# TensorE issues one stage of a hybrid decoder in the order of tracing: the MLP of the last layer's first token group, beside the end of an RWKV-7 recurrence

## The chip, the cores and the metric

One core of a Trainium2 chip runs the whole kernel. The metric is device time in microseconds (us) of one execution. A core has a matrix engine (TensorE, PE in the profile; its weight loads are listed apart as PEld), a vector engine (VectorE, DVE), a scalar engine (ScalarE, ACT), a general engine (GpSimd, POOL) and a queue engine (SyncE, SP). They run beside each other, each through its own list of instructions, strictly in the order of that list, and wait for one another by semaphores. An instruction that waits holds everything behind it on its engine.

## The reference

The model has two layers over 1040 prompt tokens (1024 and 16 learned ones put ahead of them) and 8 single decode tokens, with 1024 features. Layer 0 mixes tokens by a convolution, layer 1 by the RWKV-7 recurrence; each is followed by an MLP with 4096 hidden features. What matters here is the second layer from its recurrence on:

```
def _wkv7_step(S, inp):
    r_t, w_t, k_t, v_t, kk_t, a_t = inp
    sa = jnp.einsum('bhvk,bhk->bhv', S, -kk_t)
    S = (S * w_t[:, :, None, :] + sa[..., None] * (kk_t * a_t)[:, :, None, :]
         + v_t[..., None] * k_t[:, :, None, :])
    y = jnp.einsum('bhvk,bhk->bhv', S, r_t)
    return S, y
...
    yn = ((y - mu) * lax.rsqrt(var + GN_EPS)).reshape(B, T, D_MODEL)
...
    out = ((yn + bonus).astype(h.dtype) * g) @ w_o
...
def _sqrelu_mlp(h, w_in, w_out):
    return jnp.square(jax.nn.relu(h @ w_in)) @ w_out
```

There are 16 heads of 64 x 64 states. The 8 decode tokens take one step each from states that are inputs.

## The kernel before, in words

Features lie on the 128 partitions, tokens along the free axis. Every large product is done in three passes: activations and weights are split into a high and a low part, and high x high, high x low and low x high are summed in PSUM (L187, L188, L189). One output block of 128 features, called a column here, takes 8 blocks of input features times 3 passes, 24 matmuls of 128x128 weights by the tokens of a group. `dense` issues them. ScalarE casts the raw weights to the high part (L157), GpSimd subtracts for the low part (L162).

The recurrence goes in chunks of 64 tokens. A chunk is a chain of small products on TensorE with VectorE, ScalarE and GpSimd between them: A (L1168, products within the chunk), gg and po (L1206, in 32x32 pieces), W (L1236), U (L1252), S (L1261, the new state) and Y (L1268, L1271, the outputs), and transposes bT (L1229). gg, po, W, U and S are 16 matmuls each, Y is 32. Each piece needs the vector work on the piece before it: `w` (L1238), `p` (L1245), `uv` (L1253, L1254), `sv` (L1282). Triangular inverses for four chunks at a time are made on VectorE (`inverses`, L1127 and L1128). After the chunks `norm_gate` normalises and gates the outputs and writes them to `d_z` in DRAM, where the output projection reads them (transposes `yn`, L1388).

The last layer's output projection and MLP go by token groups. The stage in question is that of the first, 328 tokens, and it starts before the recurrence has ended: chunks 12 to 16 are still to come. `mixer_out` (L1441 on) loads the eight z parts (L1449), splits them into high and low (L140, L141), runs eight columns of the projection (`ps_oo`) and adds them to the residual (L1453). Then `mlp` (L300 on) takes the row sums (`st_m`, L231), the normalised input `m_h`, `m_l` (L269, L270), 32 columns of the first product (`ps_in`; on VectorE `r`, L327) and 16 x 8 blocks of the second (`out`, added to `h` at L340).

Between them stands other work. At fixed points (half-way through `dense`, after a column, after an `out` block) the code calls `fill`, which draws the next pieces from two streams at set rates: the recurrence (`until`), and the decode step followed by the norm gates. `decode_step` (L1317 on) first transposes the decode tokens' vectors on TensorE (`pdd`, L1327), copies them (L1330), writes them to `d_dec` and reads them back as `dq` (L1334), and then does 16 pieces of nine VectorE operations each (L1349 to L1357) on states loaded by SP's queue (L1346).

All of that gives the order of tracing. It isn't yet the order of the engines: the framework plays the traced program against a model of the engines, and each engine's instructions are issued in the order in which that model would start them, by readiness and by priority (the recurrence's priority is raised in `until`). So in before the pieces of the recurrence stand wherever the model had them ready, often one small matmul between two dense ones. Accumulators are PSUM banks from pools of fixed size (4 for the dense products, 3 for the recurrence, 1 for the others); weights pass through 5 raw buffers and 5 split ones.

Of the kernel before, what the change touches and what calls it, by code (L numbers as in the profile page):

```python
# [48 lines left out]
def hybrid_step(tc, x_prompt, x_sample, state_conv, state_shift, state_wkv, meta_tokens,  # L49
# [8 lines left out]
    nc = tc.nc  # L58
    ctx = ExitStack()
    with ctx:  # L60
# [77 lines left out]
        def split(hi, lo, src, eng_lo):  # L138

            nc.scalar.copy(hi, src)  # L140
            eng_lo.tensor_sub(lo, src, hi.bitcast(F32))  # L141
# [7 lines left out]
        def load_w(src, shape, name, eng_lo, tag="w", raw=None):  # L149

            a, b = shape
            if raw is None:
                raw = load_raw(src, shape, name)
            nb = cur["bufs"][tag]
            hi = cur["wsp"].tile([P, 8 * P], F32R, name=f"{name}_hi", tag=tag + "h", bufs=nb)
            lo = cur["wsp"].tile([P, 8 * P], F32R, name=f"{name}_lo", tag=tag + "l", bufs=nb)
            nc.scalar.copy(hi[:, :a * b], raw[:, :a * b])  # L157

            step = 2 * P if eng_lo is nc.gpsimd else a * b
            for c in range(0, a * b, step):  # L160
                cs = slice(c, min(c + step, a * b))
                eng_lo.tensor_sub(lo[:, cs], raw[:, cs], hi[:, cs].bitcast(F32))  # L162
            v = lambda t: t[:, :a * b].rearrange("p (a b) -> p a b", a=a)
            return v(hi), v(lo)
# [5 lines left out]
        def load_col(w, m, name, eng_lo, tag="w"):  # L170
            return load_w(col_src(w, m), (KT, P), name, eng_lo, tag)
# [13 lines left out]
        def mm3(ps, w, act, first, last):  # L185

            nc.tensor.matmul(ps, w[0], act[0], start=first, stop=False)  # L187
            nc.tensor.matmul(ps, w[1], act[0], start=False, stop=False)  # L188
            nc.tensor.matmul(ps, w[0], act[1], start=False, stop=last)  # L189

        def bank(name, tag="mm"):
            return cur[tag].tile([P, 512], F32, name=name, tag=tag)

        def dense(w, act, n, name, fill=None):
            ps = bank(f"ps_{name}")
            for k in range(KT):
                mm3(ps[:, :n], (w[0][:, k, :], w[1][:, k, :]), (act[0][:, k, :n], act[1][:, k, :n]), k == 0, k == KT - 1)
                if fill and k == KT // 2 - 1:
                    fill()
            return ps  # L200
# [5 lines left out]
        def tt(name, tag):  # L206
            return cur["tmp"].tile([P, cur["n"]], F32, name=name, tag=tag)
# [95 lines left out]
        def mlp(layer, groups, lag, eng_w, eng_h, fill=None, done=None):  # L303


            w_in, w_out = w_mlp_in[layer], w_mlp_out[layer]
            nj = DFF // P
            hid = {}

            def load_in(j):  # L310
                return load_col(w_in, j, f"wi{layer}_{groups[0][0]}_{j}", eng_w)

            def load_out(b):

                for i in range(2):
                    src = w_out[2 * b * P:(2 * b + 2) * P, i * 4 * P:(i + 1) * 4 * P].rearrange("(j p) c -> p j c", p=P)
                    yield load_w(src, (2, 4 * P), f"wo{layer}_{groups[0][0]}_{b}_{i}", eng_w)

            def inp(j, w, group):
                gn, hv, n, ah, al, rs, hid_pool = group  # L320
                if j % 2 == 0:
                    hid[gn, j // 2] = [hid_pool.tile([P, 2, cur["wide"]], F32R, name=f"h{q}{layer}{gn}_{j}", tag=f"h{q}") for q in "hl"]
                hh, hl = hid[gn, j // 2]
                ps = dense(w, (ah, al), n, f"in{layer}_{j}_{gn}", fill)
                with tc.high_priority(offset=HR):
                    r = tt(f"r{layer}_{j}_{gn}", "t1")
                    nc.vector.scalar_tensor_tensor(r[:, :n], ps[:, :n], 0.0, rs[:, :n], op0=ALU.max, op1=ALU.mult)  # L327
                    s = tt(f"s{layer}_{j}_{gn}", "t2")
                    nc.scalar.activation(s[:, :n], r[:, :n], AF.Square)  # L329
                    split(hh[:, j % 2, :n], hl[:, j % 2, :n], s[:, :n], eng_h)  # L330

            def out(b, i, w, group):
                gn, hv, n, ah, al, rs, hid_pool = group
                hh, hl = hid[gn, b]
                for m in range(4):
                    ps = bank(f"out{layer}_{b}_{gn}_{4 * i + m}")
                    for j in range(2):
                        mm3(ps[:, :n], [part[:, j, m * P:(m + 1) * P] for part in w], (hh[:, j, :n], hl[:, j, :n]), j == 0, j == 1)
                    with tc.high_priority(offset=HA):
                        nc.vector.tensor_add(hv[:, 4 * i + m, :], hv[:, 4 * i + m, :], ps[:, :n])  # L340
                    if fill:
                        fill()

            def outs(b):
                for i, w in enumerate(load_out(b)):
                    for group in groups:
                        out(b, i, w, group)

            last = nj - 1
            for j in range(last):  # L350
                w = load_in(j)
                for group in groups:
                    inp(j, w, group)
                b, odd = divmod(j - lag, 2)
                if b >= 0 and odd:
                    outs(b)
                if fill:
                    fill()
            for b in range((last - lag) // 2, nj // 2 - 1):
                outs(b)  # L360
            w, wo = load_in(last), list(load_out(nj // 2 - 1))
            for group in groups:
                inp(last, w, group)
                for i in range(2):
                    out(nj // 2 - 1, i, wo[i], group)
                if done and group is not groups[-1]:
                    done(group[0])

        with ExitStack() as l0:
# [6 lines left out]
            actp = [pool(l0, f"actp0{i}", 1) for i in range(2)]  # L376
            residp = [pool(l0, "resid00", 1)]
# [253 lines left out]
            with ExitStack() as s:  # L631
# [3 lines left out]
                fill, rest = filler(8 * KT, ([ranked(CV0, conv(0)), ranked(CV0, ln_silu(0))], EARLY * (15 * KT // 2 + 2 + 2 * MW + KT)))  # L635
# [43 lines left out]
            hidp = pool(l0, "hidp0", 2)  # L679
# [751 lines left out]
        with ExitStack() as l1:  # L1431
            open_weights(l1, 5, {"w": 5}, "f")
            open_tmp(l1, N2, "2", 3)
            residp = pool(l1, "resid1", 1)
            actp = pool(l1, "actp1", 1)
            hidp = pool(l1, "hidp1", 2)
# [5 lines left out]
            def mixer_out(g, residp, actp, fill, add):  # L1442
                lo, n = G2[g]
                h1 = hl[g] = residp.tile([P, KT, cur["wide"]], F32, name=f"h1_{g}", tag="h")
                nc.sync.dma_start(h1[:, :, :n], d_h[:, :, lo:lo + n])
                z = new_act(actp, f"z{g}", cur["wide"])
                for p in range(KT):
                    t = tt(f"zr{g}{p}", "t1")
                    nc.sync.dma_start(t[:, :n], d_z[:, p, lo:lo + n])  # L1449
                    split(z[0][:, p, :n], z[1][:, p, :n], t[:, :n], nc.vector)  # L1450
                for m in range(KT):
                    ps = dense(load_col(rwkv_w_o[0], m, f"wo{g}_{m}", nc.gpsimd), z, n, f"oo{g}_{m}", fill)
                    nc.vector.tensor_add(h1[:, m, :n], h1[:, m, :n], ps[:, :n])  # L1453
                    add(m, h1[:, m, :n])
                    fill()
# [57 lines left out]
            def group(g, actp, hidp, sums):  # L1513
                n = G2[g][1]
                hv = hl[g][:, :, :n]
                return (g, hv, n, *mlp_in(actp, hv, n, 1, f"m1{g}", sums), hidp)
# [3 lines left out]
            fill, rest = filler(2 * KT + MLP_POINTS,  # L1520
                                ([until(NCH - 1)], FA * CHUNK_WAIT * (NCH - 1 - st["done"])),
                                ([decode_step(), norm_gates(GN_OF[1]), ng2], NGA))
            add, sums = sums_of(0)
            mixer_out(0, residp, actp, fill, add)
            mlp(1, [group(0, actp, hidp, sums)], 2, nc.gpsimd, nc.vector, fill)
            for _ in rest:
                pass
            lw.close()
            outp = pool(l1, "outp", 1)
            cur["wide"] = max(n for lo, n in G2[1:])  # L1530
# [2 lines left out]
            fill, rest = filler(2 * KT, ([ng2], NGB))  # L1533
            add, sums = sums_of(1)
# [6 lines left out]
            fill, rest = filler(2 * KT + MLP2_POINTS, ([ranked(FN, final(0))], FB))  # L1541
            add, sums = sums_of(2)
# [3 lines left out]
            def done(g):  # L1546
                end.append(filler(KT, ([final(g)], 24)))
# [38 lines left out]
```

## Time and profile before

| | us |
|---|---|
| three runs | 2887.63, 2895.84, 2894.62; median 2894.62 |
| the profiled execution | 2896.42 |
| its span (first to last instruction) | 2894.7 |
| the changed stage in it, from the first `ps_oo` matmul to that of the next group | 1855.5 to 2313.7 |
| the mixing stage ahead of it, as counted in the text | 1236 to 1849 |

Times in rows count from the start of the span. A row of the timeline has start, duration, engine, line, operation, output and inputs by the program's names, shape and number of equal instructions in a row; what stands in brackets is the idle time before it and what ended it. Matmuls overlap in their pipeline, so the time that one costs is the distance between two starts, not its duration. The granted clock (PEclk) is the share of TensorE's full speed that it was allowed in that stretch.

### The profile page before, as it was taken

The page shows a single profiled execution, that of the slowest core. Times are in us where ns is not written, and L with a number is a line of the kernel's source. Part 1 is how long each engine was busy: PE and PEld are TensorE (multiplying, and loading weights), DVE is VectorE, ACT ScalarE, POOL GpSimd, SP SyncE. Part 2 cuts the span into 40 slices and gives each one's busy share as a digit, 9 for nine tenths or more (in the row PEclk, how much of TensorE's full clock was granted, in tenths as well). Part 3 has the DMA queues.
Part 4 walks back from the last instruction along what each step waited for, and adds up shares of the span by engine and source line. Part 5 has one row for each costly group of instructions (what it writes and reads, how often), then busy time and mean ns, then how long its engine had stood idle before and what let it go on. Part 6 is the DMA issues. An engine that isn't in the chain of part 4 may idle for free.

```text
span 2894.7 us, 51574 instructions
## 1 busy us (share of the span) xinstructions
PE 2781.4 (96%) x19594; PEld 2573.7 (89%) x19594; DVE 1785.7 (62%) x3618; ACT 1187.1 (41%) x2233; POOL 1436.8 (50%) x1983
## 2 busy tenths in 40 slices
PE   8999999999999899999999999879999999999998
PEld 8988999999999898777877877777779999999998
DVE  5999999994454544336765555597345654444444
ACT  5546444543454332333445444443234552222223
POOL 6677778887788772000100111365246883343432
PEclk9999999999999999999999999889899999999999
DMA  6563544454444643687767767854336642222211
GB/s 181 171 184 95 154 139 132 137 178 138 138 145 146 189 151 109 183 213 202 183 184 202 180 159 181 206 143 126 95 109 198 192 148 87 70 66 74 66 59 41
DMA packets 649654, 416.42 MB, mean 144 GB/s; under 512 B 126184, under 2 KB 600360, under 8 KB 649406
## 3 DMA queue, kind: packets, MB, share of 16 engines
q1 hardware_dynamic: 643164, 410.20, 50.3%
q10 hardware_dynamic: 6018, 2.89, 0.4%
q8 instruction: 155, 2.54, 0.4%
q14 instruction: 93, 0.76, 0.1%
q0 software_dynamic: 224, 0.03, 0.0%
HBM read 345.60 MB, written 68.37 MB: 143 GB/s over the span
## 4 chain that ended last, share of the span: by engine, by line
PE 75%; DVE 9%; POOL 6%; DMA 4%; issue 3%; ACT 2%; SPq 0%; DVEq 0%; ACTq 0%; POOLq 0%
PE out L187 7%; PE out L189 7%; PE out L188 7%; PE ps_in L187 7%; PE ps_in L189 7%; PE ps_in L188 7%; PE pk L845 4%; POOL wo_lo L162 3%; PE pr L845 3%; PE pv L845 3%; POOL wi_lo L162 2%; PE A L1168 2%; DVE cv L504 1%; PE U L1252 1%; PE ps_g L187 1%
## 5 line engine op out<-in xcount | busy, mean ns | idle before, releaser
L162 POOL TENSOR_TENSOR wo_lo<-wo_raw,wo_hi 128x256 fp32r<-128x256 f32 x736 | 565.3, 800 | 329.6 <-ACT wo_hi L157 301.6
L162 POOL TENSOR_TENSOR wi_lo<-wi_raw,wi_hi 128x256 fp32r<-128x256 f32 x640 | 489.0, 796 | 293.6 <-ACT wi_hi L157 253.0
L187 PE MATMUL out<-hh,wo_hi 128*128 128x352 f32 (+2 forms) x1536 | 507.2, 330 | 20.4 <-DVE r L327 9.0
L340 DVE TENSOR_TENSOR h<-h,out 128x352 f32<-128x352 f32 (+2 forms) x768 | 386.4, 510 | 220.4 <-PE out L189 219.9
L187 PE MATMUL ps_in<-m_h,wi_hi 128*128 128x352 f32 (+2 forms) x1536 | 502.4, 327 | 12.7 <-ACT m_h L269 12.1
L189 PE MATMUL out<-hl,wo_hi 128*128 128x352 f32 (+2 forms) x1536 | 497.8, 327 | 5.6 <-DVE hl L141 5.6
L188 PE MATMUL out<-hh,wo_lo 128*128 128x352 f32 (+2 forms) x1536 | 502.1, 327 | 0.0
L188 PE MATMUL ps_in<-m_h,wi_lo 128*128 128x352 f32 (+2 forms) x1536 | 501.2, 327 | 0.0
L189 PE MATMUL ps_in<-m_l,wi_hi 128*128 128x352 f32 (+2 forms) x1536 | 500.4, 326 | 0.0
L504 DVE SCALAR_TENSOR_TENSOR cv<-u,wdw,cv 128x352 f32<-128x352 f32 (+2 forms) x720 | 376.9, 573 | 0.7
L157 ACT CAST wi_hi<-wi_raw 128x1024 fp32r<-128x1024 f32 x160 | 168.0, 1050 | 399.9 <-PE out L189 191.7
L157 ACT CAST wo_hi<-wo_raw 128x1024 fp32r<-128x1024 f32 x184 | 192.9, 1050 | 321.6 <-PE out L189 158.4
L187 PEld LDWEIGHTS out<-hh,wo_hi 128*128 128x128 f32 x1536 | 293.7, 191 | 28.3 <-DVE h L340 11.0
L187 PEld LDWEIGHTS ps_in<-m_h,wi_hi 128*128 128x128 f32 x1536 | 292.4, 190 | 17.1 <-ACT m_h L269 12.5
L189 PEld LDWEIGHTS out<-hl,wo_hi 128*128 128x128 f32 x1536 | 292.9, 192 | 9.4 <-DVE hl L141 7.1
L188 PEld LDWEIGHTS out<-hh,wo_lo 128*128 128x128 f32 x1536 | 293.6, 191 | 2.9
L189 PEld LDWEIGHTS ps_in<-m_l,wi_hi 128*128 128x128 f32 x1536 | 292.3, 190 | 2.9
L188 PEld LDWEIGHTS ps_in<-m_h,wi_lo 128*128 128x128 f32 x1536 | 291.9, 190 | 3.0
L327 DVE SCALAR_TENSOR_TENSOR r<-ps_in,rs_m 128x352 f32<-128x352 f32 (+2 forms) x192 | 98.5, 515 | 263.7 <-PE ps_in L189 260.0
L141 DVE TENSOR_TENSOR hl<-s,hh 128x352 fp32r<-128x352 f32 (+2 forms) x192 | 140.4, 732 | 99.4 <-ACT hh L140 99.1
L329 ACT ACTIVATE s<-r 128x352 f32<-128x352 f32 (+2 forms) x192 | 93.9, 491 | 133.0 <-DVE r L327 132.8
L845 PE MATMUL pv<-mx,wv_raw 128*128 128x256 f32 (+2 forms) x512 | 124.9, 398 | 5.5 <-ACT rk L1029 5.5
(350 smaller groups left out, 4925.3 us busy)
## 6 DMA issues: line engine op xcount, KB each, us to landing
wi_raw<-in_w_mlp_in_dram SPq DMA_DIRECT2D x160, 512.0 KB
wo_raw<-in_w_mlp_out_dram SPq DMA_DIRECT2D x160, 512.0 KB
wk_raw<-in_rwkv_w_k_dram SPq DMA_DIRECT2D x32, 512.0 KB
wr_raw<-in_rwkv_w_r_dram SPq DMA_DIRECT2D x32, 512.0 KB
wv_raw<-in_rwkv_w_v_dram SPq DMA_DIRECT2D x32, 512.0 KB
d_ab<-ab SPq DMA_DIRECT2D x32, 512.0 KB
pg_raw<-in_conv_w_pw_dram SPq DMA_DIRECT2D x24, 512.0 KB
pa_raw<-in_conv_w_pw_dram SPq DMA_DIRECT2D x24, 512.0 KB
```

What stands on the lines that cost most here:

```text
L141: eng_lo.tensor_sub(lo, src, hi.bitcast(F32))
L157: nc.scalar.copy(hi[:, :a * b], raw[:, :a * b])
L162: eng_lo.tensor_sub(lo[:, cs], raw[:, cs], hi[:, cs].bitcast(F32))
L187: nc.tensor.matmul(ps, w[0], act[0], start=first, stop=False)
L188: nc.tensor.matmul(ps, w[1], act[0], start=False, stop=False)
L189: nc.tensor.matmul(ps, w[0], act[1], start=False, stop=last)
L327: nc.vector.scalar_tensor_tensor(r[:, :n], ps[:, :n], 0.0, rs[:, :n], op0=ALU.max, op1=ALU.mult)
L329: nc.scalar.activation(s[:, :n], r[:, :n], AF.Square)
L340: nc.vector.tensor_add(hv[:, 4 * i + m, :], hv[:, 4 * i + m, :], ps[:, :n])
L504: nc.vector.scalar_tensor_tensor(acc[m][:, :n], ug[:, m, j:j + n], wdw[:, m, j:j + 1], acc[m][:, :n], op0=ALU.mult, op1=ALU.add)
L845: nc.tensor.matmul(ps[:, :n], w[:, k, :], act[k], start=k == 0, stop=k == KT - 1)
L1168: nc.tensor.matmul(ps[:, i * 2 * P:(i + 1) * 2 * P], bk[:, j + i, :], xa[:, j + i].rearrange("p q x -> p (q x)"), start=True, stop=True)
```

## The change

The calls that trace the stage are put under `manual_schedule` for TensorE: its instructions of this stage are issued in the order in which they are traced. VectorE, ScalarE, GpSimd and the DMA queues are ordered by the model as before, and before and behind the stage so is TensorE.

```
             add, sums = sums_of(0)
-            mixer_out(0, residp, actp, fill, add)
-            mlp(1, [group(0, actp, hidp, sums)], 2, nc.gpsimd, nc.vector, fill)
-            for _ in rest:
-                pass
+            with tc.manual_schedule(engines={nc.tensor.engine}):
+                mixer_out(0, residp, actp, fill, add)
+                mlp(1, [group(0, actp, hidp, sums)], 2, nc.gpsimd, nc.vector, fill)
+                for _ in rest:
+                    pass
             lw.close()
```

The order of TensorE at the start of the stage becomes: half of column 0 of the projection; gg and bT of chunk 12 and the first two `pdd` transposes; the rest of column 0; half of column 1, two `pdd`, and so on to the last two `pdd` behind column 3; W, po, U, S and Y of chunk 12 each in one block between halves of columns; after column 7 the row sums, and only then the first product's columns, one after the other. In before, the first columns were taken side by side as the z parts came in, and the `pdd` transposes were issued in the stage ahead.

## The prediction

> **What bounds the kernel now.** I read the head of the page first, then the chain that ended last.
>
> ```profile
> span 2894.7 us, 51574 instructions
> PE 2781.4 (96%) x19594; PEld 2573.7 (89%) x19594; DVE 1785.7 (62%) x3618; ACT 1187.1 (41%) x2233; POOL 1436.8 (50%) x1983
> ...
> PE 75%; DVE 9%; POOL 6%; DMA 4%; issue 3%; ACT 2%; SPq 0%; DVEq 0%; ACTq 0%; POOLq 0%
> ```
>
> TensorE carries three quarters of the chain, so time taken from TensorE is time taken from the kernel, unless another engine is late there. But a busy TensorE need not be a fast one. The second view is the table by windows: the mixing stage ahead, then the changed stage in four parts. The columns are PE, PEld, DVE, ACT and POOL busy with their instructions, the granted clock, the DMA share and GB/s.
>
> ```profile
> 1236.00:1849.00 613.00, 582.85 (x5770) 479.81 (x5769) 352.91 (x863) 272.94 (x719) 67.86 (x149) 0.98 0.73 187
> 1871.70:1910.00 38.30, 33.99 (x268) 31.64 (x268) 36.98 (x82) 15.00 (x27) 22.61 (x26) 0.94 0.68 151
> 1910.00:2040.50 130.50, 119.75 (x805) 98.72 (x805) 106.05 (x221) 45.34 (x83) 68.33 (x82) 0.87 0.49 134
> 2040.50:2200.00 159.50, 159.50 (x1056) 121.42 (x1055) 64.61 (x132) 53.01 (x107) 58.22 (x72) 0.89 0.38 104
> 2200.00:2309.00 109.00, 107.97 (x720) 106.83 (x718) 72.41 (x129) 57.49 (x100) 92.95 (x117) 1.00 0.72 216
> ```
>
> Until 2040 the stage is shared: VectorE is busy 37.0 of 38.3 us, then 106 of 130.5, with the decode step and the chunk's inverses. From 2040 to 2200 TensorE is busy without a gap and yet passes 1056 matmuls in 159.5 us, fewer per us than in the last 109 us, which have none of the recurrence. All other engines are under half busy there. Why, the timeline of TensorE shows.
>
> ```profile
> 2085.08 0.31 PE L188 MATMUL out<-hh,wo_lo 128*128 128x328 f32 x1
> 2085.23 0.31 PE L189 MATMUL out<-hl,wo_hi 128*128 128x328 f32 x1
> ...
> 2086.32 0.33 PE L1236 MATMUL W<-sv,xa 128*64 128x64 f32 x2
> 2086.57 0.41 PE L188 MATMUL out<-hh,wo_lo 128*128 128x328 f32 x1
> 2086.92 0.33 PE L1236 MATMUL W<-sv,xa 128*64 128x64 f32 x2
> ...
> 2149.12 1.15 PE L1236 MATMUL W<-sv,xa 128*64 128x64 f32 x32
> 2150.20 0.69 PE L1206 MATMUL po<-p,gg 32*32 32x32 f32 x32
> ```
>
> Dense matmuls (128x328) start 0.15 us apart (2085.08, 2085.23). One small W instruction (two records) set between two dense ones makes the pair 0.60 us long (2086.32 to 2086.92). The same W's in one block (16 instructions, 32 records) take 2150.20 - 2149.12 = 1.08 us, 0.068 each. So a lone small matmul costs 0.60 - 0.15 - 0.07 = 0.38 us more than one in a block. At a low clock it is worse:
>
> ```profile
> 2003.81 0.64 PE L187 MATMUL out<-hh,wo_hi 128*128 128x328 f32 x1
> 2004.38 0.31 PE L1206 MATMUL gg<-x,no 32*32 32x32 f32 x2
> 2004.63 0.64 PE L188 MATMUL out<-hh,wo_lo 128*128 128x328 f32 x1
> ```
>
> The pair is now 0.82 us (2003.81 to 2004.63).
>
> **The change part by part.** No instruction is added or taken away: in the program's order each engine issues the same operations. What moves is TensorE's order; the other engines' orders are still the scheduler's and shift along with it. In tracing order each recurrence piece (gg, W, po, U, S, Y: 16 instructions each, Y 32) stands in one block, with some 70 dense matmuls between blocks, where before had them singly between dense ones. I split the stage at the first A product of chunk 15, behind which the same instructions are left in both orders.
>
> ```profile
> 2039.82 1.02 PE L1168 MATMUL A<-xa,bk 128*128 128x256 f32 x4
> ...
> 2313.72 0.32 PE L187 MATMUL ps_oo<-z_h,wo_hi 128*128 128x352 f32 x1
> ```
>
> *Second part*, from there to the next group's first matmul: 273.9 us in before. Its work, put together from rows:
>
> ```profile
> 1887.53 2.00 PE L1168 MATMUL A<-xa,bk 128*128 128x256 f32 x8
> 1889.18 0.50 PE L187 MATMUL ps_oo<-z_h,wo_hi 128*128 128x328 f32 x1
> ...
> 2146.49 0.60 PE L1388 MATMUL yn<-ident,ey 128*128 128x128 f32 x4
> ```
>
> 47 weight columns of 24 dense matmuls, 1128 x 0.15 = 169.2. S 48, Y 96, W 32, U 32 instructions, 208 x 0.068 = 14.1. gg and po, 64 at about 0.04 (the po row: 0.69 us with its tail for 16) = 2.6. A, 16 instructions, four of which (eight records) took 1889.18 - 1887.53 = 1.65 us: 6.6. Transposes (bT 16, yn 48, state 16) at about 0.11 ((0.60 - 0.27) / 3 in the yn row) = 8.8. Sum 201.3 us; 72.6 us of before are no work. The granted clock explains part of it: 0.89 over 159.5 us lacks 17.5 us of pulses. The other 55 are some 140 lone matmuls at 0.38.
>
> In blocks the 55 go. Two things stay. First, the clock: the mixing stage runs the same pieces in blocks, and it had 0.98 over 613 us and 12 chunks, 12 us or 1 a chunk. Here it is 0 at best and 17.5 at worst; I take 6, near the mixing row, since dense blocks keep TensorE as busy as in the last window (1.00). Second, waits: a piece that isn't ready now holds the dense matmuls behind it. Before shows few of them:
>
> ```profile
> PE S L1261 <- DVE uv L1253: 0.8, 1, 0.8
> PE gg L1206 <- DVE x L1182: 0.6, 1, 0.6
> ```
>
> With 70 dense matmuls (10 us) between blocks, and VectorE under half busy, an answer (a copy of under 1 us and an add) is mostly there; eight blocks at 0.5 give 4 (0 to 20). After: 201.3 + 6 + 4 = 211.3, so 62.6 us less. No other engine takes over: in the windows POOL is busy 58 + 93 = 151 us and DVE 65 + 72 = 137, against 211. DMA would be at 0.52 x 274 / 211 = 0.68 (0.52 is the mean of the last two windows by length), under the 0.72 that the last window carried at full speed.
>
> *First part*, up to 2039.82, is where the change also makes things later.
>
> ```profile
> L1330 ACT COPY dst<-pdd x4: 365/365/370, 1830.3 to 1844.9; 48x256 f32<-48x256 f32 x4
> ...
> 1853.94 0.40 ACTq L1334 DMA_DIRECT2D dq<-d_dec  x1
> ...
> 1871.70 0.41 DVE L1349 TENSOR_TENSOR t<-Sdec,dq 128x256 f32<-128x256 f32 x1
> ...
> 1883.58 0.50 DVE L141 TENSOR_TENSOR z_l<-zr,z_h 128x328 fp32r<-128x328 f32 x1 [1.10 <-ACT z_h L140]
> ```
>
> The decode step's four transposes (pdd) were drawn ahead of the stage and copied by 1844.9; its VectorE work began at 1871.70. In tracing order the last of them stands behind four whole columns of the output projection. The first column needs the last z part (1884.1) and now nothing of columns 1 to 3 can pass it; then 72 x 0.15 = 10.8 us, W and po 1.8, and 2 for clock and turns: 1900. From the last copy to the load of dq took 9 us (1844.9 to 1853.94), so VectorE starts the decode at about 1910, 38 us later. ACT's queue holds these small DMAs, SP's the decode states; both wait ready and hold nobody long. Also the row sums (st_m) now stand ahead of the MLP's first product.
>
> ```profile
> 1903.87 1.89 PE L1168 MATMUL A<-xa,bk 128*128 128x256 f32 x8
> 1917.81 0.64 PE L187 MATMUL ps_in<-m_h,wi_hi 128*128 128x328 f32 x1 [12.05 <-ACT m_h L269]
> 1918.25 0.48 PE L188 MATMUL ps_in<-m_h,wi_lo 128*128 128x328 f32 x1
> ...
> L1128 DVE TENSOR_TENSOR ni<-ni,tt 128x210 f32<-128x210 f32 (+14 forms) x21 | 10.1, 483 | 0.1
> L1127 DVE TENSOR_TENSOR tt<-ni 128x220 f32<-128x220 f32 (+14 forms) x20 | 9.4, 470 | 0.0
> L141 DVE TENSOR_TENSOR z_l<-zr,z_h 128x328 fp32r<-128x328 f32 x5 | 2.4, 486 | 1.1 <-ACT z_h L140 1.1
> ```
>
> That wait of 12 us exists already, so it moves (to about 1928) rather than is added. What sets the end is VectorE: from 1871.7 to 2040.5 it was busy 37.0 + 106.0 = 143.0 us. The inverses (10.1 + 9.4) and z parts (2.4) run ahead of the late decode, so 121 are left. Idle, it had 25.8 us in that stretch, mostly waits for products that TensorE passed slowly:
>
> ```profile
> DVE h L340 <- PE out L189: 11.2, 5, 6.7
> DVE r L327 <- PE ps_in L189: 7.1, 2, 5.3
> ```
>
> With TensorE quicker I keep 6. So 1910 + 121 + 6 = 2037, 3 us ahead of 2040 (between +9 with no idle time and -17 with all 25.8). TensorE's own need, 600 dense at 0.15 and 28 us of small pieces, 118 us, lies beside it.
>
> *Sum*: 62.6 + 3 = 65.6. The profiled execution took 2896.42 us (span 2894.7 and 1.7 around it): 2831. That run is 1.8 above the median of the three, 2894.62, so I say 2829.
>
> A rule of the Trainium skill speaks against the change. "TensorE: Matmul & The Clock Gate", section "HAM oscillation — how this bites in real kernels", has the clock halved after each wait longer than an activity window, given there as about 3.4 us. The trace agrees once (after 12.05 us of idle time the dense matmuls at 1918.25 stand 0.27 us apart); but 2003 to 2005 is as slow with no idle time at all, which waits alone don't explain. By the rule, the second rival below is likelier than I make it.
>
> **The rivals.** *Waits eat half of it.* VectorE keeps its 25.8 us (-17 instead of +3), the eight blocks of the second part wait 1.5 us each rather than 0.5 (8 more), and the clock stays as now (11 more): 2829 + 20 + 8 + 11 = 2868. For it: VectorE is the fuller engine until 2000 and starts the decode late. Against: it is under half busy after 2040.
>
> *In-order hops make it slower.* In the first part each of the W, po, U and S blocks of chunks 12 to 14 waits for a copy that is queued on VectorE behind a decode piece, and all dense work stands behind the block. One piece:
>
> ```profile
> 1928.23 0.41 DVE L1349 TENSOR_TENSOR t<-Sdec,dq 128x256 f32<-128x256 f32 x1
> ...
> 1933.30 0.42 DVE L1357 TENSOR_REDUCE yd<-t 128x4 f32<-128x256 f32 x1
> ```
>
> 5.5 us, and some 11 dense matmuls at 0.27 behind the wait, 1.3 more: 6.8 x 12 hops = 82 us, 2829 + 82 = 2911. It turns slower from 65.6 / 12 = 5.5 us a hop. For it: TensorE had something else to issue at all these places before. Against: the copies can be ordered ahead of decode pieces on VectorE, and while TensorE waits VectorE does work that it owes anyway; even with nothing beside each other, 118 + 121 us end at about 2110.
>
> *The lone matmuls weren't the cost.* If weights paced the stage (DMA, POOL), the order would change nothing: 2895. Against: the last window moves 216 GB/s at clock 1.00 and the slow one 104.
>
> **How the numbers follow.** The forecast with its own range (2813 with VectorE never idle, no waits and a full clock, and 5 for the spread of runs, which was -7 to +1 in before: 2808; up to 2850): 0.60. Waits eat half (2850 to 2886): 0.24. Slower hops: 0.12. No change: 0.04. The range 2808 to 2878 leaves out the last two and a little of the second. About 0.3% is what a measurement of this kernel can tell from no change; faster by more than that 0.84, within it 0.04, slower 0.12.
>
> **What would show it.** Right: S, Y, W and U rows of 32 records without dense rows between them; the next group's ps_oo some 65 us earlier; a stretch of about 211 us from the first A of chunk 15 to it; a clock near 0.97 there. The decode's first VectorE row near 1910. Wrong: TensorE rows with idle times of several us ahead of U or S and VectorE named as releaser; a clock under 0.9 in spite of blocks; or A of chunk 15 after 2060, which would put the loss on the late decode.

## The result and the profile after

The changed kernel takes 2841.93 us (median of four runs, 2840.69 to 2845.53) against 2895.23 of before (2887.63 to 2899.05): a ratio of 0.9825, with an interval from 0.9805 to 0.9845. That is 53 us less. I had said 66 less, 2829; the time lies in the range, 13 us above the forecast.

The head of the page and the chain of the changed kernel answer to the first lines shown of before:

```profile
span 2840.2 us, 51589 instructions
PE 2687.1 (95%) x19594; PEld 2530.3 (89%) x19594; DVE 1787.1 (63%) x3618; ACT 1188.8 (42%) x2233; POOL 1431.8 (50%) x1983
...
PE 72%; DVE 13%; DMA 7%; issue 3%; POOL 3%; ACT 2%; SPq 1%; DVEq 0%; ACTq 0%; POOLq 0%
```

TensorE is busy 94 us less with the same 19594 matmuls, but the span is only 54.5 us shorter, and VectorE and DMA have a larger share of the chain. So TensorE got quicker and then waited for others.

The windows show where. First before, then the changed kernel; each has the stage cut at the first A of chunk 15 and ended at the next group's first `ps_oo`.

```profile
1855.50:2039.80 184.30, 168.00 (x1202) 142.11 (x1201) 152.42 (x325) 63.43 (x117) 98.90 (x118) 0.87 0.58 151
2039.80:2313.70 273.90, 271.88 (x1801) 232.58 (x1801) 142.38 (x270) 114.23 (x212) 154.43 (x192) 0.94 0.52 150
```

```profile
1851.40:2011.90 160.50, 132.75 (x1248) 123.46 (x1249) 145.69 (x313) 66.05 (x120) 96.79 (x118) 0.90 0.65 165
2011.90:2260.40 248.50, 215.49 (x1804) 208.54 (x1802) 150.83 (x286) 115.18 (x216) 150.05 (x188) 0.94 0.61 173
```

The first part went from 184.3 to 160.5 us and the second from 273.9 to 248.5, 49 us together; the stage began 4 us earlier (1851.4 for 1855.5), and what follows it takes 579.8 us (581.0). In the second part TensorE has 33 us without work, where before had 2.

The blocks are as they should be. The timeline of TensorE in the changed kernel:

```profile
2039.33 0.31 PE L189 MATMUL out<-hl,wo_hi 128*128 128x328 f32 x1
2039.57 1.15 PE L1236 MATMUL W<-sv,xa 128*64 128x64 f32 x32
2040.65 0.69 PE L1206 MATMUL po<-p,gg 32*32 32x32 f32 x32
2041.27 0.42 PE L187 MATMUL out<-hh,wo_hi 128*128 128x328 f32 x1
...
2044.86 0.31 PE L189 MATMUL out<-hl,wo_hi 128*128 128x328 f32 x1
2045.10 1.15 PE L1252 MATMUL U<-w,p 64*64 64x64 f32 x32
```

W and po of a chunk together are through in 1.7 us, and U comes 24 dense matmuls later without a wait. The waits are elsewhere. These are the longest of TensorE in the second part (engine, operation, line and what it waited for; us, times, longest):

```profile
PE yn L1388 <- DVE ey L1384: 11.3, 3, 6.1
PE yn L1388 <- issue: 9.6, 2, 5.4
PE Y L1268 <- DVE nr L1176: 2.7, 1, 2.7
PE pfs L1289 <- DVE fs L1284: 2.6, 1, 2.6
PE A L1168 <- DVE fs L1279: 2.3, 1, 2.3
```

21 us stand at `yn`, the norm gates' transposes, which the prediction didn't price; the recurrence has only 8.

To see all of TensorE's time at once I took every distance between two starts of matmuls in the stage and set it against the distance that the same pair has in a block at the full clock. What is over is put down to a wait where it is over 1.5 us, to the clock where the granted clock was half, and else to turns between dense and small matmuls. So a turn that was made at half clock stands in the row of the half clock, and the shares of the two rows are good to a few us.

| us in the stage | before | changed | gates on constants | priority instead |
|---|---|---|---|---|
| work | 314.9 | 317.5 | 317.5 | 315.5 |
| turns and lone small matmuls | 82.8 | 17.9 | 15.7 | 21.2 |
| half clock | 44.7 | 18.1 | 15.7 | 8.7 |
| waits | 15.7 | 55.6 | 30.4 | 26.6 |
| sum | 458 | 409 | 379 | 372 |

The last two columns are experiments below. The change took 65 us of turns and 27 of half clock and gave 40 back as waits.

The half clock has two origins here. In the second part of before it came three times, 34 us in all, with TensorE issuing without a pause; in the changed kernel it came six times, 31 us in all, each time at a wait of 2.6 to 6.1 us or just behind it, four of them at `yn`. One of each, first before, then the changed kernel around the longest wait at `yn`:

```profile
2067.60:2081.30 13.70, 13.70 (x56) 10.19 (x55) 0.34 (x1) 3.43 (x7) 0.48 (x1) 0.50 0.31 77
```

```profile
2147.20:2154.10 6.90, 4.11 (x16) 4.11 (x17) 5.40 (x10) 3.12 (x7) 3.40 (x4) 0.51 0.36 110
```

So the second part's mean granted clock is 0.94 in both kernels. By the starts it cost 21 us in before and 10 in the changed kernel, since part of the half-clock time there was spent waiting anyway.

### The profile page after: what moved, and what is told of

It is laid out like the page before. It is cut to its first block, busy times and chain, and to the rows that moved or that the text cites. A ratio compares the mean times of both kernels' runs of the same rounds, so it can differ in the third digit from the quotient of the medians.

```text
span 2840.2 us, 51589 instructions
## 1 busy us (share of the span) xinstructions
PE 2687.1 (95%) x19594; PEld 2530.3 (89%) x19594; DVE 1787.1 (63%) x3618; ACT 1188.8 (42%) x2233; POOL 1431.8 (50%) x1983
## 4 chain that ended last, share of the span: by engine, by line
PE 72%; DVE 13%; DMA 7%; issue 3%; POOL 3%; ACT 2%; SPq 1%; DVEq 0%; ACTq 0%; POOLq 0%
PE out L187 7%; PE out L189 7%; PE out L188 7%; PE ps_in L188 7%; PE ps_in L187 7%; PE ps_in L189 7%; PE pk L845 4%; PE pr L845 3%; PE pv L845 2%; PE A L1168 2%; DVE cv L504 1%; POOL wi_lo L162 1%; DMA d_z<-ez 1%; DVE hl L141 1%; DVE h L340 1%
## 5 line engine op out<-in xcount | busy, mean ns | idle before, releaser
L162 POOL TENSOR_TENSOR wo_lo<-wo_raw,wo_hi 128x256 fp32r<-128x256 f32 x736 | 559.6, 792 | 293.0 <-ACT wo_hi L157 285.7
L188 PE MATMUL ps_in<-m_h,wi_lo 128*128 128x352 f32 (+2 forms) x1536 | 494.9, 322 | 0.0
L141 DVE TENSOR_TENSOR hl<-s,hh 128x352 fp32r<-128x352 f32 (+2 forms) x192 | 146.9, 766 | 107.5 <-ACT hh L140 107.2
```

## The experiments

The theory after the result: lone small matmuls cost TensorE turns and clock, blocks take that away, and the fixed order has a price of its own, mostly at the norm gates. The rivals: the gain comes from something else that the order does (the projection's columns, the late decode), and the waits are only where the slack of another bound shows.

**Gates on constants.** The transposes of the later gates read the identity tile, so the normalisation is left out of the result.

```
- nc.tensor.transpose(pt[:, ...], y[:n, k * P:(k + 1) * P], ident[:n, :n])
+ nc.tensor.transpose(pt[:, ...], (y[:n, k * P:(k + 1) * P] if i in GN_OF[0] else ident[:n, :]), ident[:n, :n])
```

> The changed kernel, but the norm gates' transposes (yn) of the later token groups read a constant tile instead of the normalised outputs (the normalisation is left out of what is computed), so TensorE has nothing to wait for there. Theory (the 12 yn blocks, each at a fixed place in TensorE's list, hold the dense matmuls behind them for 22 us because the gate's chain of loads, VectorE and ScalarE steps isn't done): the waits at yn go and the time falls by 15 to 22 us, to 2820 to 2827. Rival (the waits sit at yn by chance and VectorE or the weights pace the second part): the idle time moves to other matmuls, 2838 to 2843.

2815.72 us, ratio 0.9718 (0.9684 to 0.9753) to before on that chip. The waits that were at `yn` are gone, and no others took their place. TensorE's waits behind the first A of chunk 15:

```profile
PE Y L1268 <- DVE nr L1176: 2.5, 1, 2.5
PE A L1168 <- DVE fs L1279: 2.3, 1, 2.3
PE pfs L1289 <- DVE fs L1284: 1.9, 1, 1.9
PE out L187 <- ACT hh L140: 1.6, 1, 1.6
```

The theory holds, and its price was set too low: the kernel gains about 26 us by the medians of two chips, some 31 by the ratios. The 21 us of waits aren't all of it; without them the second part takes 219 us for 248.5, and its clock rises from 0.94 to 0.98, with 7 us at half clock for 31:

```profile
2017.60:2236.60 219.00, 208.07 (x1804) 202.10 (x1803) 150.81 (x285) 114.58 (x216) 155.59 (x191) 0.98 0.67 196
```

The rival falls: neither VectorE nor the weights paced the second part.

**Decode early.** The first five pieces of the decode step are drawn ahead of the stage.

```
+            dec = decode_step()
+            for _ in range(5):
+                next(dec)
...
-                                ([decode_step(), norm_gates(GN_OF[1]), ng2], NGA))
+                                ([dec, norm_gates(GN_OF[1]), ng2], NGA))
```

> The changed kernel, with the decode step's transposes, their write and the load of dq drawn ahead of the manually ordered stage. Theory (VectorE with the late decode bounds the first part; it began at 1899.6 and VectorE was busy 110.1 of the next 112.3 us): the decode starts near 1875, the first A of chunk 15 comes 10 to 20 us earlier than 2012, and the time falls by 8 to 15, to about 2830. Rival (the z parts and the row sums set the first part's time, TensorE waited 16 and 7 us for them): under 3 us.

2837.95 us, ratio 0.9796 (0.9760 to 0.9833); the interval takes in the changed kernel's 0.9825, so nothing can be told from no gain. The decode's VectorE work does begin early, at 1865.9, yet the first A of chunk 15 comes at 2029.1, 172.9 us after the stage's start, where the changed kernel took 160.5. VectorE was idle for 22 us of it:

```profile
1856.20:2029.10 172.90, 139.10 (x1244) 128.84 (x1245) 150.94 (x332) 66.70 (x123) 99.14 (x118) 0.85 0.62 164
```

The cut doesn't part the same work in both, though: VectorE has 332 instructions ahead of it here and 313 in the changed kernel. What is behind it is shorter by more:

```profile
2029.10:2261.20 232.10, 211.37 (x1800) 205.78 (x1799) 139.82 (x266) 113.12 (x208) 150.51 (x191) 0.95 0.62 177
```

The stage as a whole takes 405.0 us for 409.0, and in a second profile of the changed kernel (below) 404.3. So no loss by the late decode can be told, and my own theory of it fell: a decode begun 34 us earlier didn't bring the first A of chunk 15 earlier.

**Priority instead of a fixed order.** The kernel before, without the manual order; the recurrence's priority alone is raised in this stage, so that the model puts a ready piece whole ahead of dense matmuls.

```
-        RE = 0
+        RE = 1000
```

> The kernel before, no manual order; only the priority of the recurrence raised by 1000 in this stage, so that a piece that is ready goes whole ahead of dense matmuls: 62 changes between small and dense in TensorE's list of the stage instead of 462 (40 in the changed kernel). Theory (blocks instead of lone small matmuls are the gain, the fixed order only costs waits): 2825 to 2845. Rival (the order of tracing itself, or the later decode, is the gain): 2880 or more.

2807.73 us, ratio 0.9696 (0.9654 to 0.9738): faster than the changed kernel, and below my own expectation. (The raise in `until` is by `RE`, which is 0 in before.) The list of TensorE has 62 changes between small and dense instead of 462, and the table above shows the same drop in turns and the lowest loss by the clock. TensorE's longest waits in this stage:

```profile
PE ps_in L187 <- ACT m_h L269: 13.2, 1, 13.2
PE out L187 <- DVE r L327: 5.0, 5, 2.8
PE A L1168 <- DVE nr L1176: 2.4, 2, 2.2
```

No `yn` is among them (0.5 us in all): where the model may set a later matmul ahead, a gate that isn't ready holds nobody. The first row is the wait that took 12 us in before. With this run the rival that the order of tracing as such makes the gain is out. The priority acts on all engines, so how much of the lead is VectorE's and ScalarE's order isn't separated.

**Manual order for the MLP alone.** `mixer_out` is taken out of the `with` block.

```
-            with tc.manual_schedule(engines={nc.tensor.engine}):
-                mixer_out(0, residp, actp, fill, add)
+            mixer_out(0, residp, actp, fill, add)
+            with tc.manual_schedule(engines={nc.tensor.engine}):
```

> Manual order for the MLP and the rest alone; the output projection's columns in the model's order as before (58 changes between small and dense). Theory: the second part's gain stays, the first part gains as much from blocks and loses the waits for z parts (16 us): 2830 to 2845. Rival (the gain of 28 us up to the first A of chunk 15 comes from the projection's order): 2860 to 2875.

2842.32 us, ratio 0.9806 (0.9766 to 0.9845), as the changed kernel. The rival is out: the projection's order brings nothing. Nor does leaving it to the model save the 16 us of waits for z parts, since TensorE then waits at the row sums, which stay ahead of the MLP (the stage's longest waits):

```profile
PE st_m L231 <- POOL acc_m L253: 11.9, 1, 11.9
PE yn L1388 <- DVE ey L1384: 11.6, 5, 4.0
PE yn L1388 <- issue: 10.5, 2, 6.5
PE st_m L231 <- DVE acc_m L253: 8.9, 1, 8.9
```

**The price of a lone matmul by itself.** 144 extra 64x64 matmuls in a stretch that has no recurrence: once behind each dense matmul, once in blocks of six.

```
                        nc.tensor.matmul(ps[:, :n], ww[0], aa[0], start=j == 0, stop=False)
+                       small(3 * j)
                        nc.tensor.matmul(ps[:, :n], ww[1], aa[0], start=False, stop=False)
+                       small(3 * j + 1)
                        nc.tensor.matmul(ps[:, :n], ww[0], aa[1], start=False, stop=j == 1)
+                       small(3 * j + 2)
```

> The changed kernel with 144 extra 64x64 matmuls on constants (their results are not used), one behind each dense matmul of the last three rows of blocks of the first group's second MLP product. To be compared with the next run, which has the same 144 in 24 blocks of six. Theory (each turn from dense to small and back costs TensorE about 0.38 us over a matmul in a block): 120 turns more, 46 us more than the next run; more still if the clock falls in that stretch, as it did in the stage before. Rival (the lone matmuls of before were slow because TensorE waited for others there): the two runs within 8 us.

> The same 144 extra 64x64 matmuls in 24 blocks of six, one behind each block of six dense matmuls. Theory: 24 turns at 0.4 and 120 more matmuls at 0.07, 18 us over the changed kernel (2860). Rival: as the run before, within 8 us of it.

Lone: 2952.0 us, 1.0220 (1.0196 to 1.0244). In blocks: 2858.05, 0.9890 (0.9868 to 0.9912). The blocks came as forecast, the lone ones at 94 us over them, twice the forecast; by the distances between starts 88 of them stand at half clock. The timeline of the lone run says why:

```profile
2222.14 0.33 PE L340 MATMUL px<-ident 64*64 64x64 f32 x2
2222.39 0.42 PE L347 MATMUL out<-hh,wo_lo 128*128 128x328 f32 x1
2222.74 0.33 PE L340 MATMUL px<-ident 64*64 64x64 f32 x2
...
2250.43 0.47 PE L340 MATMUL px<-ident 64*64 64x64 f32 x2
2250.84 0.64 PE L347 MATMUL out<-hh,wo_lo 128*128 128x328 f32 x1
2251.41 0.47 PE L340 MATMUL px<-ident 64*64 64x64 f32 x2
```

A pair starts at 0.60 us (2222.14 to 2222.74), the price that was read from before, and 28 us later takes 0.98. The windows of the same run:

```profile
2222.10:2245.00 22.90, 22.90 (x85) 13.66 (x84) 3.14 (x6) 2.93 (x4) 6.19 (x9) 0.64 0.16 47
2245.00:2363.00 118.00, 117.55 (x398) 73.94 (x397) 26.05 (x46) 20.14 (x37) 20.82 (x27) 0.56 0.19 56
```

and of the run with blocks:

```profile
2230.90:2280.00 49.10, 47.09 (x480) 40.17 (x480) 22.56 (x40) 15.91 (x28) 24.09 (x32) 0.97 0.45 131
```

The clock is 0.56 for 118 us in which TensorE had no idle time worth the name, and 0.97 in blocks. So lone matmuls bring the half clock without any wait. Whether the turn itself does it, or only that fewer matmuls pass (3.4 per us here, 9.8 in blocks), these runs don't separate.

**A later place for the gates' transposes.** The pause behind them is moved ahead of them.

```
-                yield 2.5
+                yield 5 if i not in GN_OF[0] else 2.5
                 pt = bank(f"yn{i}_{hf}", "w")
...
                 nc.sync.dma_start(d_z[:, ps_, lo:lo + n], fm(z))
-                yield 2.5
+                yield 0 if i not in GN_OF[0] else 2.5
```

> The changed kernel with the pause behind a norm gate's transposes moved ahead of them (5 and 0 units in place of 2.5 and 2.5), so that a third more dense matmuls stand in TensorE's list between a gate's load and its transposes. Theory (the gate's chain is longer than the distance in the list): about half of the 22 us of waits at yn go, 2828 to 2836. Rival (the gates are held by their own single buffers, so that the next gate's chain starts later by as much): 2838 to 2845.

2832.91 us, ratio 0.9816 (0.9781 to 0.9852). The time alone lies in the theory's range, but the kernel before was also faster on this chip (2887.04), and by the ratio the run isn't to be told from the changed kernel (0.9825). The waits at `yn` are 15.7 us (8.0 and 7.7) for 20.9, a quarter less and not half. So neither side is settled. The chain of waits in the changed kernel shows one thing that a later place doesn't mend:

```profile
2140.63 6.24 DMA d_z<-ez
...
2146.95 0.64 ACT eq L1376
...
2147.61 0.69 DVE ems L1381
...
2149.25 0.70 DVE ey L1384
...
2149.99 1.11 PE yn L1388 x4
```

The square of the next gate (`eq`) goes into the single buffer that the gate before still writes to DRAM from (`ez`, 6.24 us); behind it VectorE, and behind that `yn` with all dense matmuls. A second buffer would test it; no run has one.

**Priority in the mixing stage too.**

```
-        RC = 0
+        RC = 1000
```

together with the raised `RE`.

> The kernel before with the recurrence's priority raised by 1000 in the mixing stage too, not only in the stage of the first group (no manual order). Theory (lone small matmuls are the cost wherever they stand): the mixing stage of before has some 30 lone ones of 109 stretches, worth up to 11 us; 2797 to 2806. Rival (recurrence pieces ahead of the mixing work there delay what VectorE and ScalarE need): 2808 or more.

2818.54 us, ratio 0.9753 (0.9733 to 0.9773), about 16 us worse by the ratio than raising it in the one stage. The mixing stage has as many changes between small and dense in both traces (219), so the run doesn't test lone matmuls there. The stage began 12 us later (1865.6 for 1853.2) and itself took as long (371.8 us for 371.9), so the loss lies ahead of it; which work was delayed there isn't shown.

**One chip for both, and two variants.** The changed kernel and the raised priority once more:

> The changed kernel once more, beside the next runs on one chip: 2838 to 2846 by every theory.

> The kernel before with the recurrence's priority raised by 1000 in the stage of the first group, once more, to set it against the changed kernel on one chip. Theory (blocks give the gain, the fixed order only adds waits, 26 us by the run with gates on constants): 25 to 40 us under the changed kernel. Rival (its lead was the chip's): within 10 us of it.

2836.41 us, 0.9813 (0.9791 to 0.9836), and 2805.15 us, 0.9699 (0.9677 to 0.9722): 31 us apart, as the second of the two texts expected (25 to 40); the changed kernel came 1.6 us under the range of the first. The kernel with one raised number beats both kernels of this case.

With `NG = 1000` beside it, for the norm gates:

> As the run before, with the norm gates' priority raised by 1000 too. Theory (without a fixed order the gates hold nothing up): within 6 us of the run before. Rival (the gates still pace the second part): 8 us less or more.

2813.16 us, 0.9728 (0.9705 to 0.9751), 8 us above the run before it and not below, and each of its runs is above each of the other's. So the gates don't pace that kernel. Neither side had expected a loss, and what causes it isn't shown.

A third of the density for the lone matmuls, `small(j)` behind every third dense one:

> The changed kernel with 48 extra 64x64 matmuls, one behind every third dense matmul of the stretch in which the earlier run had 144. Theory (a lone small matmul costs 0.45 us at the full clock, and the clock halves only where they stand behind every dense one): 22 us over the changed kernel, granted clock over 0.9 in the stretch. Rival (lone small matmuls halve the clock at this density too): 36 to 45 us over it, clock near 0.6.

2869.4 us, 0.9922 (0.9899 to 0.9945), 33 us over the changed kernel on that chip, between both forecasts. In its trace 40 us pass at the full clock, then it is halved once, for 24 us:

```profile
2236.00:2290.00 54.00, 52.23 (x247) 40.48 (x246) 20.15 (x36) 17.08 (x29) 21.33 (x29) 0.78 0.40 113
```

48 turns at 0.45 are 22 us, and 24 us at half the clock lose 12: by this estimate 34. At this density the clock fell late and once; at one behind each dense matmul it fell after 6 us and was down for 41 us and more at a time.

## Why the prediction came out as it did

*What bounds the kernel.* Right in the cause. By the distances between starts the second part of before has 201 us of work, 52 of turns and 21 of half clock, where the prediction had 201.3, 55 and 17.5; in the changed kernel 7 and 10 of the turns and the half clock are left. The price of a lone matmul, 0.38 us over one in a block, was measured by itself (0.60 us a pair at the full clock). Two readings were loose. The "some 140 lone matmuls" were 55 divided by 0.38 and not a count; the timeline has 163 stretches of small matmuls between dense ones there, about 125 of them a single instruction. And 1056 matmuls in 159.5 us are not fewer per us than 720 in 109, both are 6.6; what differs is that only 413 of the first are dense (2.6 per us), and 690 of the second (6.3).

*The clock.* I kept it as a term of its own, 17.5 us of before, of which 6 would stay, beside 55 of lone matmuls. In the second part the half clock cost 21 us in before and 10 in the changed kernel. The size was near, but the cause wasn't seen, and the clock of 0.97 that I gave as a sign didn't come: it is 0.94 as in before. In before, where the second part has 2 us of waits in all, the half clock came with the lone matmuls, as in the lone run. In the changed kernel it came with the waits, and mostly went with those at `yn` (the run with gates on constants). The Trainium skill's rule on waits, weighed in the prediction ("TensorE: Matmul & The Clock Gate", "HAM oscillation — how this bites in real kernels"), has gaps of over about 3.4 us bring the half clock. The changed kernel agrees at its four long waits at `yn`, of about 4 to 6.1 us; but the clock also fell behind waits of 2.6 and 2.7 us there, and in the second part of before with no wait.

*Waits in the second part.* This is the step that failed: "eight blocks at 0.5 give 4". I counted only the recurrence's blocks. The norm gates' twelve `yn` blocks stand in the same list, behind a chain of a DMA, two VectorE reductions, ScalarE and a single buffer. TensorE waited 30 us, 21 of it at `yn`. So the second part took 248.5 us where I had 211.3, and gained 25 for 63; of the 37 us between, 26 are waits, 7 turns that stayed and 4 the clock.

*The first part.* Also wrong, the other way: 24 us were gained where I had 3, and the stage began 4 earlier. VectorE is full as said: from the decode's first row it is busy 110.1 of 112.3 us.

```profile
1899.61 0.41 DVE L1349 TENSOR_TENSOR t<-Sdec,dq 128x256 f32<-128x256 f32 x1
...
1899.60:2011.90 112.30, 98.22 (x955) 92.06 (x954) 110.08 (x233) 50.30 (x91) 71.32 (x84) 0.95 0.60 155
```

All three numbers of that sum were too high: the start (1910, measured 1899.6), the work ahead of chunk 15 (121, measured 110; the last decode piece, some 5 us, moved behind it) and the idle time (6, measured 2). VectorE's idle time in the whole part fell from 31.9 us (184.3 - 152.4) to 14.8: its waits for dense products (11.2 and 7.1 us in before, shown in the prediction) are gone from the list of its waits. The longest one in the changed kernel is for a DMA:

```profile
DVE x L1182 <- DMA p<-d_p: 5.9, 1, 5.9
```

The late decode that I charged for cost nothing that can be told, as the second experiment showed. There VectorE stood idle for 22 us in spite of the early start, so VectorE isn't the only bound of this part; what else holds it wasn't separated.

*The rivals.* "Waits eat half of it" came in part: not as VectorE's idle time, but the granted clock of the second part did stay as it was, and the waits came at the gates, more of them than the rival had. "In-order hops" didn't: in the first part, where it set them, TensorE's waits at recurrence pieces sum to 4 us, in the second to 8. "The lone matmuls weren't the cost" is out by the lone run. That the forecast came within 13 us was luck: two errors, 37 us too much in the second part and 25 too little ahead of it, nearly met.

## What to carry to other kernels

In this kernel small tiled matmuls between dense ones had to stand in blocks, and the profile shows whether they do by the distances between starts, not by busy time. If a scheduler scatters them, try raising the priority of what they belong to before fixing the whole order: a fixed order also pins every matmul of a slow side chain, and each of those holds all that stands behind it. When a wait list is priced, go through every producer of that engine in the stretch, not only the one that the change is about.

## What the runs showed of the hardware

The granted clock fell to half with TensorE busy all the time: 0.56 over 118 us, 117.55 of them busy, with one 64x64 matmul behind each 128x328 one, and 0.97 with the same matmuls in blocks of six. At one behind every third it was 0.78. At half clock the pair took 0.98 us for 0.60. In the second part of the changed kernel the clock fell to half at six waits of TensorE or just behind them, of 2.6 to 6.1 us; with the waits at `yn` taken away the mean clock of that part went from 0.94 to 0.98.
